# Projection weights of a two-layer encoder: one split per layer kept in DRAM and reloaded as pairs, against a split at each use

## The chip, the cores and the metric

The kernel runs on one core of one Trainium2 chip. The metric is the device time of one execution in microseconds (us); a lower time is better.

## What is computed

Two sequences (x_prompt and x_sample, 1024 tokens of width 1024 each) go through the same two layers. Per layer:

```
(shift, scale, gate) = silu(c) @ W_ada + b_ada
h = RMSNorm_pre(x) * (1 + scale) + shift
P = h @ W_in                      # 1024 -> 32 tiles of 128 columns
A: latent attention, B: RWKV-7, C: Mamba-2 SSD, D: gated DeltaNet   # four mixers on columns of P
x = x + gate * RMSNorm_post(concat(A, B, C, D) @ W_out)
```

All arrays are float32. The weights of a layer are the same for both sequences.

## The kernel before, in words

There are four units of work, (sequence 0, layer 0), (1, 0), (0, 1), (1, 1). Each has an input projection (`stage_in`), four mixers (`mixers`) and an output projection (`stage_out`; the last unit's is `stage_out_last`). While the mixers of one unit run, the projections of its neighbours are spread between them: `ahead`, `behind` and `spread` give their instructions a priority in the middle of the mixers', and a scheduler then writes each engine's queue. Every engine, and SP, which issues all DMAs, works through its own queue in order.

The projections are done in float32 accuracy with three float32r matmuls per block: each operand is the sum of a high part (rounded to float32r) and a low part (the rest). For the activations these are hh and hl, made once per half of a sequence. For the weights they are wh and wl. `in_tile` (line 302) makes one tile of P, 128 columns of W_in by 512 tokens (half `hf`): for each half of the contraction (4 blocks of 128 rows) a tile w of 128 x 512 float32 (256 KB) is loaded (line 309), ScalarE (ACT) casts it to wh (line 327) and VectorE (DVE) subtracts to wl (line 329), both of them in `split_w` and with raised priority (`urgent`). Twelve matmuls follow (line 458, in `paced`), hh by wh, hl by wh, hh by wl for each of the four blocks. `out_tiles` (line 332) does the same for W_out with 256 columns per matmul. w has two buffers, wh and wl three each (GB, GL).

`paced` ties each run of 5 (TK) or 8 (TO) of these matmuls to a memset of a token on GpSimd (line 462), which the next run waits for.

A tile of P, `st`, goes to DRAM; the mixers load it from there (G, cvi, zz and others). Lines that the prediction speaks of: the convolution of mixers C and D is line 638 (DVE, cva) with 634 and 636 (ACT), its activation 640 (ACT, cvt), and 1025 squares it for the norm in D, whose sums PE takes with line 590.

Each weight tile is used four times per layer, by two sequences and two halves. So there are 2 layers x 32 tiles x 2 halves of the contraction x 4 uses = 512 loads and splits for W_in, and 2 x 4 column blocks x 4 x 4 = 128 for W_out, 640 in all. By W_D, W_B and W_REST the 32 tiles of W_in are dealt in three parts; each unit runs the parts for one half of the sequence and then for the other. The stretches of the trace that the prediction names are W_REST (19 tiles) of four parts: 339 to 529 us of sequence 0 in layer 0 (first use of these tiles), 1318 to 1487 of sequence 1 in layer 0, 2581 to 2732 of sequence 0 in layer 1 (first use), 3729 to 3892 of sequence 1 in layer 1. The place from 3660 to 3680 us lies in the parts before the last of these.

Of the kernel before, what the change touches and what calls it, by code (L numbers as in the profile page):

```python
# [21 lines left out]
D = 1024  # L22
MIX = 1800
EA = 60
GK = 4
GB = 3
EB = 60
TK = 5
TO = 8
ED = 90  # L30
GL = 3
SB = 3
NPT = 8
EC = 60
T = 1024
# [73 lines left out]
class Body:  # L109
    def __init__(self, ctx, tc, A, outs, sl=None):  # L110
        self.tc, self.nc, self.A, self.outs = tc, tc.nc, A, outs
        self.n = 0
        self.side = "left"
        self.span = None
        nc = tc.nc
        self.cp = ctx.enter_context(tc.tile_pool(name="cp", bufs=1))
        self.dr = ctx.enter_context(tc.tile_pool(name="dr", bufs=1, space=DRAM))
        self.banks = 3
        self.held = None
        self.token = self.t(self.cp, [1, 1], tag="token")  # L120
        self.gate, self.run = None, 0
        self.ident = self.const(self.cp, "ident")
        self.blk = self.const(self.cp, "blk")
        self.bsel = self.const(self.cp, "bsel")
        self.cc = self.t(self.cp, [128, 4], tag="cc")
        nc.vector.memset(self.cc[:, 0:1], -0.5)
        nc.vector.memset(self.cc[:, 1:2], EPS)
        nc.vector.memset(self.cc[:, 2:3], 0.5)
        nc.vector.memset(self.cc[:, 3:4], 1.0)
        self.mhalf, self.eps, self.phalf, self.one1 = (self.cc[:, i:i + 1] for i in range(4))  # L130
# [127 lines left out]
                    for j in range(2):  # L258
                        nc.vector.tensor_scalar(L.gsc[:, k0 + j, :], ps2[:, 2 * j:2 * j + 2], 1.0, L.pp("gpre", k0 + j), ADD, MUL)

    def stage_in(self, s, L, l, xsrc, Pd, parts=((0, W_ORDER), (1, W_ORDER))):

        for hf, names in parts:
            if self.held is None or self.held[0] != (Pd, hf):
                self.spread()
                hh = self.t(self.pj, [128, 8, 512], F32R, tag="hh")
                hl = self.t(self.pj, [128, 8, 512], F32R, tag="hl")
                self.norm_in(s, L, xsrc, hf, hh, hl)
                self.held = (Pd, hf), hh, hl
            for name in names:  # L270
                self.spread()
                self.in_tile(l, name, hf, *self.held[1:], Pd)
# [28 lines left out]
    def in_tile(self, l, name, hf, hh, hl, Pd):  # L301
# [3 lines left out]
        ps = self.t(self.pps, [128, 512], tag="pj")  # L305
        for k in range(8):
            if k % 4 == 0:
                w = self.t(pj, [128, 4, 128], tag="w", bufs=2)
                self.dma(w, self.A["w_in"][l, ci][:, k * 128:k * 128 + 512].rearrange("p (k c) -> p k c", k=4))
            if k % GK == 0:  # L310
                with self.urgent():
                    wh, wl = self.split_w(w[:, k % 4:k % 4 + GK], [128, GK, 128])
            for i, (a, b) in enumerate(((wh, hh), (wh, hl), (wl, hh))):
                self.paced(TK, ps[0:M], a[:, k % GK, 0:M], b[:, k, :], dict(start=(k == 0 and i == 0), stop=(k == 7 and i == 2)))
        st = self.t(pj, [128, 512], tag="st", bufs=SB)
        with self.urgent():
            if name[0] == "z":
# [3 lines left out]
                nc.scalar.copy(st[0:M], ps[0:M])  # L321
        self.dma(Pd[ci * 128:ci * 128 + M, hf * 512:(hf + 1) * 512], st[0:M])

    def split_w(self, w, shape):
        nc, pj = self.nc, self.pj
        wh = self.t(pj, shape, F32R, tag="wh", bufs=GB)
        nc.scalar.copy(wh, w)  # L327
        wl = self.t(pj, shape, F32R, tag="wl", bufs=GL)
        nc.vector.tensor_tensor(wl, w, wh.bitcast(F32), SUB)  # L329
        return wh, wl  # L330

    def out_tiles(self, l, ch, hh, hl, kqs, at=lambda kq: kq):

        nc, pj = self.nc, self.pj
        pss = [self.t(self.pps, [128, 2, 256], tag="pj") for _ in range(2)]
        for n, kq in enumerate(kqs):
            w = self.t(pj, [128, 2, 256], tag="w", bufs=2)
            self.dma(w, self.A["w_out"][l, ch, kq // 2][:, (kq % 2) * 512:(kq % 2) * 512 + 512].rearrange("p (k c) -> p k c", k=2))
            with self.urgent():
                wh, wl = self.split_w(w, [128, 2, 256])  # L340
            for i in range(4):
                ps = pss[i // 2][:, i % 2]
                c = slice(i * 128, (i + 1) * 128)
                for k in range(2):
                    a, b = hh[:, at(kq) * 2 + k, c], hl[:, at(kq) * 2 + k, c]
                    first, last = n == 0 and k == 0 and i % 2 == 0, n == len(kqs) - 1 and k == 1
                    for m, (u, w2) in enumerate(((a, wh), (a, wl), (b, wh))):
                        self.paced(TO, ps, u, w2[:, k], dict(start=first and m == 0, stop=last and m == 2, skip_group_check=True))
        return pss

    def stage_out(self, s, L, l, xsrc, od, dst):
# [1253 lines left out]
    def full(self):  # L1605
# [11 lines left out]
        def run_in(u, *parts):  # L1617
            s, l = units[u]
            if u not in P:
                P[u] = self.t(self.dr, [NWT * 128, 1024], tag="P", bufs=2)  # L1620
            self.stage_in(s, L[l], l, src(s, l), P[u], parts)

        def run_out(u):
            s, l = units[u]
# [20 lines left out]
        def out_last(parts, ctx=None):  # L1645
            s, l = units[3]
            self.stage_out_last(s, L[l], l, src(s, l), o[3], self.outs[s], parts, ctx)

        early = (0, W_D + W_B), (1, W_D + W_B)
        late = (1, W_REST), (0, W_REST)  # L1650
        with ExitStack() as io:
# [62 lines left out]

# [12 lines left out]
```

## Time and profile before

| | us |
|---|---|
| three runs: median (lowest to highest) | 4856.7 (4849.28 to 4880.52) |
| the profiled execution | 4863.89 |
| its span, first to last instruction | 4862.1 |
| mean granted TensorE clock in it | 0.877 of full speed |

The trace is of one execution. Names are those of the program without buffer numbers; L458 is line 458. A line can be that of a helper: line 144 is every DMA issue, line 458 every paced matmul, of which pj<-hh,wl and its like belong to the input projection. SP's DMA queue is called SPq. A busy time of PE contains the latency of its matmuls, which overlap. A wait is put down to what came last.

### The profile page before, as it was taken

To read this page: it belongs to the slowest core of one execution; us is meant where nothing else is said; L and a number is where in the kernel's file an instruction comes from. 1 tells how busy PE (TensorE), PEld (TensorE's weight loads), DVE (VectorE), ACT (ScalarE), POOL (GpSimd) and SP (SyncE) were. 2 spreads that over 40 slices of the span, in tenths; PEclk is the share of its full clock that TensorE was granted. 3 is DMA by queue.
4 is the path that set the end of the run, shared out by engine and by line. 5 is a ranking of instruction groups with operands and counts; after the bars stand their busy time and mean duration, and the time that the engine had idled before them with its cause. 6 is when DMAs were issued, how large, how long until landed. Compare 5 with 4: busy or idle time off the path is not lost.

```text
span 4862.1 us, 100716 instructions
## 1 busy us (share of the span) xinstructions
PE 4303.3 (89%) x38644; PEld 3243.0 (67%) x38644; DVE 3351.1 (69%) x6837; ACT 2177.4 (45%) x4734; POOL 399.5 (8%) x2093
## 2 busy tenths in 40 slices
PE   6879798999898988998989898898989988889985
PEld 3657565767676775764767666775767766767675
DVE  2488878567688886555549869767556969857466
ACT  2444364554435453531554454454445254446233
POOL 0111010000101110000011100000011100000000
PEclk8889898998998897988989799797989988878688
DMA  4444364343543455453445354644245345365233
GB/s 146 136 146 143 99 196 145 100 114 117 164 148 121 144 162 158 129 152 100 138 144 164 113 166 132 197 140 135 70 149 177 129 135 157 111 200 146 75 100 127
DMA packets 495063, 671.79 MB, mean 138 GB/s; under 512 B 149752, under 2 KB 265976, under 8 KB 493560
## 3 DMA queue, kind: packets, MB, share of 16 engines
q1 hardware_dynamic: 494584, 665.36, 43.9%
q8 instruction: 306, 5.01, 0.4%
q14 instruction: 173, 1.42, 0.1%
HBM read 486.53 MB, written 178.57 MB: 137 GB/s over the span
## 4 chain that ended last, share of the span: by engine, by line
PE 58%; DVE 16%; DMA 14%; issue 5%; ACT 5%; SPq 1%; POOL 1%; DVEq 0%; POOLq 0%; ACTq 0%
PE pj L458 27%; PE b L824 2%; DVE iA L522 2%; PE b L1570 2%; PE b L551 2%; DMA w<-w_in 2%; PE pj L243 2%; PE b L557 1%; PE b L1557 1%; DVE wl L329 1%; DVE GT L537 1%; SPq L144 1%; PE y L1222 1%; PE b L1526 1%; PE b L590 1%
## 5 line engine op out<-in xcount | busy, mean ns | idle before, releaser
L458 PE MATMUL pj<-hh,wl 128*128 128x512 f32 (+1 forms) x2048 | 849.4, 415 | 41.9 <-DVE wl L329 28.8
L458 PE MATMUL pj<-hh,wh 128*128 128x512 f32 (+1 forms) x2048 | 854.2, 418 | 25.8 <-POOL token L462 10.2
L458 PE MATMUL pj<-hl,wh 128*128 128x512 f32 (+1 forms) x2048 | 847.4, 414 | 18.3 <-POOL token L462 18.2
L327 ACT CAST wh<-w 128x512 fp32r<-128x512 f32 x640 | 395.6, 618 | 782.6 <-PE pj L458 523.8
L329 DVE TENSOR_TENSOR wl<-w,wh 128x512 fp32r<-128x512 f32 x640 | 447.3, 700 | 253.3 <-ACT wh L327 211.7
L458 PEld LDWEIGHTS pj<-hh,wl 128*128 128x128 f32 (+1 forms) x2048 | 397.2, 194 | 148.1 <-DVE wl L329 27.6
L458 PEld LDWEIGHTS pj<-hh,wh 128*128 128x128 f32 (+1 forms) x2048 | 398.0, 194 | 128.8 <-POOL token L462 16.1
L458 PEld LDWEIGHTS pj<-hl,wh 128*128 128x128 f32 (+1 forms) x2048 | 397.8, 194 | 113.9 <-POOL token L462 26.3
L462 POOL MEMSET token<- 1x1 f32 x1613 | 143.4, 89 | 3347.0 <-PE pj L458 3342.1
L458 PE MATMUL pj<-wh,hl 128*128 128x256 f32 x896 | 270.7, 313 | 1.3 <-DVE hl L363 1.2
L1561 ACT ACTIVATE pT<-b 128x512 f32<-128x512 f32 x256 | 150.7, 598 | 262.7 <-PE b L1559 258.2
L458 PE MATMUL pj<-wh,hh 128*128 128x256 f32 x768 | 236.2, 308 | 11.5 <-ACT st L372 5.9
L458 PE MATMUL pj<-wl,hh 128*128 128x256 f32 x768 | 231.5, 302 | 3.7 <-DVE wl L329 3.7
L294 PE MATMUL pj<-c_ident,x 128*128 128x128 f32 x416 | 120.4, 393 | 122.0 <-DVE x L289 43.9
L1527 DVE TENSOR_REDUCE mx<-b 128x1 f32<-128x512 f32 x256 | 169.9, 684 | 84.1 <-PE b L1526 82.4
L638 DVE SCALAR_TENSOR_TENSOR cva<-cvi,cw,cva 128x1024 f32<-128x1024 f32 x144 | 183.7, 1278 | 46.8 <-ACT cva L634 33.8
L458 PEld LDWEIGHTS pj<-wh,hl 128*128 128x128 f32 x896 | 182.8, 208 | 17.5 <-issue 9.7
L1570 PEld LDWEIGHTS b<-VO,pT 128*64 128x64 f32 x4096 | 152.8, 144 | 52.1 <-issue 43.9
L1570 PE MATMUL b<-VO,pT 128*64 128x65 f32 x4096 | 182.5, 233 | 0.9 <-ACT pT L1561 0.9
L824 PE MATMUL b<-AR,BK 64*64 64x128 f32 x2048 | 178.4, 305 | 3.5 <-DVE G L829 3.2
L829 DVE SCALAR_TENSOR_TENSOR G<-b,Dk,mk 128x128 f32<-128x128 f32 x512 | 140.7, 341 | 53.2 <-PE b L824 52.8
L296 ACT ACTIVATE ht<-pj,shc,gsc 128x256 f32<-128x256 f32 x208 | 118.6, 570 | 126.8 <-PE pj L294 63.2
(403 smaller groups left out, 9125.1 us busy)
## 6 DMA issues: line engine op xcount, KB each, us to landing
w<-w_in SPq DMA_DIRECT2D x512, 256.0 KB
P<-st SPq DMA_DIRECT2D x248, 256.0 KB
x<-x SPq DMA_DIRECT2D x76, 512.0 KB
w<-w_out SPq DMA_DIRECT2D x128, 256.0 KB
G<-P SPq DMA_DIRECT2D x112, 256.5 KB
cvi<-P SPq DMA_DIRECT2D x48, 512.0 KB
f<-acr SPq DMA_DIRECT2D x32, 512.0 KB
bkc<-bkd SPq DMA_DIRECT2D x64, 256.0 KB
```

The costliest lines, as they stand in the source:

```text
L294: nc.tensor.transpose(ps[:, i * 128:(i + 1) * 128], xs[i][:, k * 128:(k + 1) * 128], self.ident)
L296: nc.scalar.activation(ht, ps[:, 0:256], AF.Identity, scale=L.gsc[:, k, s:s + 1], bias=L.shc[:, k, s:s + 1])
L327: nc.scalar.copy(wh, w)
L329: nc.vector.tensor_tensor(wl, w, wh.bitcast(F32), SUB)
L458: m = self.nc.tensor.matmul(*mm[:3], **mm[3]).ins
L462: t = self.nc.gpsimd.memset(self.token, 0.0).ins
L638: nc.vector.scalar_tensor_tensor(a, c[:, j:j + 1024], wt(j, i), a, MUL, ADD)
L824: nc.tensor.matmul(pss[x][self.half(x ^ a), i * 128:i * 128 + 128], BK[self.half(x), pr, c, a], AR[self.half(x), pr, c].rearrange("p a t - ...
L829: v.scalar_tensor_tensor(G[:, x, pr, c, :], pss[x][:, i * 128:i * 128 + 128], Dk[:, c, 2 * x + pr:2 * x + pr + 1], mk, MUL, MUL)
L1527: v.tensor_reduce(mx[:, n, qt:qt + 1], ps, AX.X, ALU.max, negate=True)
L1561: nc.scalar.activation(pT[kt], ps, AF.Exp)
L1570: nc.tensor.matmul(po[64 * x:64 * x + 64, i, :], pT[kt][:, o:o + 64], VO[:, kt, h, :], start=(kt == 0 and i == 0), stop=(kt == 7), skip_gr ...
```

## The change

`split_w` is replaced by `halves`. The first time that a half tile of a weight is used, w is loaded and split as before, but into one tile w2 that holds both parts (128 x 2 x 512, 512 KB), and w2 is then also written to a DRAM tile (`win`, `wout`). At the other three uses the pair is loaded from there into w2 and no engine splits anything. w2 has six buffers (WB = 6), 24 KB per partition, in the place of three wh and three wl (12 KB); w keeps two. The matmuls read w2[:, 0] for wh and w2[:, 1] for wl; their count and shapes stay. `dynamic_dma_scratch_size` of 1024 is passed at the creation of the program, where nothing was passed before. `stage_in` has a path that writes hh and hl to DRAM and loads them back; the set `twice` that selects it is empty, and no such DMA is in the program.

In counts: casts and subtractions 640 before, 160 after; loads of w 640 before, 160 after; loads of pairs 0 and 480; writes of pairs 0 and 160.

```diff
@@ constants @@
-GK = 4
-GB = 3
-GL = 3
+WB = 6
@@ Body.__init__ @@
+        self.kept = {}
+        self.wd = {(n, l): self.t(self.dr, [m, 128, 2, 512], tag=f"w{n}{l}") for l in range(DEPTH) for n, m in (("in", 2 * NWT), ("out", 16))}
+        self.spilled = {}
@@ in_tile @@
             if k % 4 == 0:
-                w = self.t(pj, [128, 4, 128], tag="w", bufs=2)
-                self.dma(w, self.A["w_in"][l, ci][:, k * 128:k * 128 + 512].rearrange("p (k c) -> p k c", k=4))
-            if k % GK == 0:
-                with self.urgent():
-                    wh, wl = self.split_w(w[:, k % 4:k % 4 + GK], [128, GK, 128])
-            for i, (a, b) in enumerate(((wh, hh), (wh, hl), (wl, hh))):
-                self.paced(TK, ps[0:M], a[:, k % GK, 0:M], b[:, k, :], dict(start=(k == 0 and i == 0), stop=(k == 7 and i == 2)))
+                w2 = self.halves(("in", l, ci, k // 4), lambda: self.A["w_in"][l, ci][:, k * 128:k * 128 + 512]).rearrange("p u (k c) -> p u k c", k=4)
+            for i, (a, b) in enumerate(((0, hh), (0, hl), (1, hh))):
+                self.paced(TK, ps[0:M], w2[:, a, k % 4, 0:M], b[:, k, :], dict(start=(k == 0 and i == 0), stop=(k == 7 and i == 2)))
...
-    def split_w(self, w, shape):
+    def halves(self, key, src):
         nc, pj = self.nc, self.pj
-        wh = self.t(pj, shape, F32R, tag="wh", bufs=GB)
-        nc.scalar.copy(wh, w)
-        wl = self.t(pj, shape, F32R, tag="wl", bufs=GL)
-        nc.vector.tensor_tensor(wl, w, wh.bitcast(F32), SUB)
-        return wh, wl
+        w2 = self.t(pj, [128, 2, 512], F32R, tag="w2", bufs=WB)
+        wf = w2.bitcast(F32)
+        if key in self.kept:
+            self.dma(wf, self.kept[key])
+            return w2
+        w = self.t(pj, [128, 512], tag="w", bufs=2)
+        self.dma(w, src())
+        with self.urgent():
+            nc.scalar.copy(w2[:, 0], w)
+            nc.vector.tensor_tensor(w2[:, 1], w, wf[:, 0], SUB)
+        kept = self.wd[key[:2]]
+        self.kept[key] = kept[key[2] * 2 + key[3]] if key[0] == "in" else kept[key[2] * 4 + key[3]]
+        self.dma(self.kept[key], wf)
+        return w2
@@ out_tiles @@
-            w = self.t(pj, [128, 2, 256], tag="w", bufs=2)
-            self.dma(w, self.A["w_out"][l, ch, kq // 2][:, (kq % 2) * 512:(kq % 2) * 512 + 512].rearrange("p (k c) -> p k c", k=2))
-            with self.urgent():
-                wh, wl = self.split_w(w, [128, 2, 256])
+            w2 = self.halves(("out", l, ch, kq), lambda: self.A["w_out"][l, ch, kq // 2][:, (kq % 2) * 512:(kq % 2) * 512 + 512]).rearrange("p u (k c) -> p u k c", k=2)
...
@@ full, kernel @@
+        twice = set()
-    nc = bacc.Bacc("TRN2", target_bir_lowering=False, num_devices=1)
+    nc = bacc.Bacc("TRN2", target_bir_lowering=False, num_devices=1, dynamic_dma_scratch_size=1024)
```

Line numbers after the change are higher by 1 at the DMA issue (145) and by 14 from `out_tiles` on (458 is 472, 640 is 654, 1025 is 1039).

The first place is ACT's queue in the last unit (sequence 1, layer 1), in the convolution of mixer D, while the projection tiles W_D and W_B of half 1 are spread between: cva and cvt are of the convolution, st is a tile of P leaving PSUM. Before:

```order
L321 COPY st_37871<-pj_37829 128x512
L634 ACTIVATE cva_40263<-cvi_40259,cw_15_114 128x1024
L327 CAST wh_37942<-w_37940 128x512
L327 CAST wh_37967<-w_37965 128x512
L321 COPY st_37916<-pj_37874 128x512
L640 ACTIVATE cvt_40268<-cva_40263 128x1024
L1024 COPY KQ_40084<-cva_40263 128x16x64
L1025 ACTIVATE cvt_40268<-cva_40263 128x1024
L327 CAST wh_37987<-w_37985 128x512
```

After:

```order
L648 ACTIVATE cva_38539<-cvi_38535,cw_19_118 128x1024
L328 COPY st_36544<-pj_36510 128x512
L654 ACTIVATE cvt_38544<-cva_38539 128x1024
L1038 COPY KQ_38360<-cva_38539 128x16x64
L1039 ACTIVATE cvt_38544<-cva_38539 128x1024
L328 COPY st_36581<-pj_36547 128x512
```

The casts are gone from this place, and the rest stands in the same order.

The second place is SP's queue in the same part of the program: w and win are weights, P_..<-st_.. stores a tile of P, cvi loads one for the convolution. Before:

```order
L144 DMA w_37761<-w_in 128x512
L144 DMA P_36722<-st_37692 128x512
L144 DMA w_37786<-w_in 128x512
L144 DMA cvi_40161<-P_36722 128x1024
L144 DMA w_37806<-w_in 128x512
L144 DMA P_36722<-st_37737 128x512
L144 DMA w_37830<-w_in 128x512
```

After:

```order
L145 DMA w_5338_36454<-win_3_62 128x1024
L145 DMA P_35510<-st_36360 128x512
L145 DMA w_5341_36474<-win_3_62 128x1024
L145 DMA cvi_38437<-P_35510 128x1024
L145 DMA w_5342_36491<-win_3_62 128x1024
L145 DMA P_35510<-st_36397 128x512
L145 DMA w_5345_36511<-win_3_62 128x1024
```

The weights stand where they stood among the other transfers, each twice as long. The running numbers tell how far ahead of the tile being stored a load stands: a tile of P takes 45 numbers before and 37 after, so w_37761 beside st_37692 is about 1.5 tiles ahead, and w_36454 beside st_36360 about 2.5.

The third place is SP's queue in the first stage, where the first tiles are split. Before:

```order
L144 DMA w_500<-w_in 128x512
L144 DMA w_521<-w_in 128x512
L144 DMA w_545<-w_in 128x512
L144 DMA hl_228<-w_ada 128x1024 x2
L144 DMA ht_205<-b_ada 2x256
```

After:

```order
L145 DMA win_1_60<-w_117_459 128x1024
L145 DMA w_505<-w_in 128x512
L145 DMA win_1_60<-w_119_480 128x1024
L145 DMA w_526<-w_in 128x512
L145 DMA win_1_60<-w_123_504 128x1024
L145 DMA w_550<-w_in 128x512
L145 DMA hl_232<-w_ada 128x1024 x2
L145 DMA ht_209<-b_ada 2x256
```

Each load of w now has the write of an earlier pair ahead of it.

On PE the matmuls of the projections stand at most some 130 places (of 9216) earlier or later among the mixers' instructions than they did, except in the last 1500 instructions of the mixers, where up to 250 come later and, at the very end, some 130 earlier.

## Rows read from the trace of the kernel before

**Rows 1.** Page, section 1: engine, busy us (share of span), x instructions.
```profile
span 4862.1 us, 100716 instructions
...
PE 4303.3 (89%) x38644; PEld 3243.0 (67%) x38644; DVE 3351.1 (69%) x6837; ACT 2177.4 (45%) x4734; POOL 399.5 (8%) x2093
```

**Rows 2.** Chain that ended last, whole program: by engine, then by line.
```profile
PE 58%; DVE 16%; DMA 14%; issue 5%; ACT 5%; SPq 1%; POOL 1%; DVEq 0%; POOLq 0%; ACTq 0%
...
by line: PE pj L458 27.1%; issue 4.8%; PE b L824 2.2%; DVE iA L522 2.2%; PE b L1570 2.0%; PE b L551 1.8%; DMA w<-w_in 1.8%; PE pj L243 1.8%; PE b L557 1.4%; PE b L1557 1.3%; DVE wl L329 1.3%; DVE GT L537 1.3%; SPq L144 1.3%; PE y L1222 1.2%
```

**Rows 3.** Page, section 5: the split's groups and their first reader.
```profile
L458 PE MATMUL pj<-hh,wl 128*128 128x512 f32 (+1 forms) x2048 | 849.4, 415 | 41.9 <-DVE wl L329 28.8
...
L327 ACT CAST wh<-w 128x512 fp32r<-128x512 f32 x640 | 395.6, 618 | 782.6 <-PE pj L458 523.8
L329 DVE TENSOR_TENSOR wl<-w,wh 128x512 fp32r<-128x512 f32 x640 | 447.3, 700 | 253.3 <-ACT wh L327 211.7
```

**Rows 4.** Waits, whole program: us in total, times, longest us.
```profile
ACT wh L327 <- PE pj L458: 523.8, 280, 9.2
...
DVE wl L329 <- ACT wh L327: 211.7, 165, 9.3
ACT wh L327 <- DMA w<-w_in: 180.2, 91, 8.8
```

**Rows 5.** Waits of SP's DMA queue, whole program, same columns.
```profile
SPq L144 <- DVE wl L329: 580.7, 232, 23.2
```

**Rows 6.** Timeline of ACT, 3660 to 3680: start, us, instruction [idle before].
```profile
3672.53 0.62 ACT L327 CAST wh<-w 128x512 fp32r<-128x512 f32 x1 [3.94 <-PE pj L458]
...
3673.53 1.06 ACT L640 ACTIVATE cvt<-cva 128x1024 f32<-128x1024 f32 x1
...
3676.84 1.05 ACT L1025 ACTIVATE cvt<-cva 128x1024 f32<-128x1024 f32 x1
```

**Rows 7.** Timeline of DVE, then of PE, same stretch and columns.
```profile
3668.86 0.68 DVE L329 TENSOR_TENSOR wl<-w,wh 128x512 fp32r<-128x512 f32 x1
3669.47 2.60 DVE L638 SCALAR_TENSOR_TENSOR cva<-cvi,cw,cva 128x1024 f32<-128x1024 f32 x2
...
3677.94 2.30 PE L590 MATMUL b<-cc,cvt 64*64 64x1 f32 x40 [3.66 <-ACT cvt L1025]
```

**Rows 8.** Windows: length, busy us (instructions) per engine, PEclk, DMA share, GB/s.
```profile
339.00:529.00 190.00, 183.25 (x1604) 145.09 (x1602) 160.87 (x312) 81.79 (x179) 20.27 (x108) 0.95 0.43 140
1318.00:1487.00 169.00, 150.50 (x1040) 118.68 (x1038) 146.75 (x261) 68.96 (x127) 13.72 (x110) 0.92 0.49 152
2581.00:2732.00 151.00, 143.01 (x940) 111.73 (x938) 143.99 (x244) 53.87 (x82) 22.72 (x107) 1.00 0.49 152
3729.00:3892.00 163.00, 150.56 (x1025) 120.20 (x1024) 156.49 (x250) 56.55 (x86) 21.25 (x108) 0.94 0.47 144
```

**Rows 9.** The chain by line in 1318 to 1487, then in 3729 to 3892.
```profile
by line: PE pj L458 34.7%; DMA w<-w_in 17.6%; issue 7.4%; DVE GT L537 5.4%; PE b L1304 3.4%; SPq L144 3.4%; PE b L1066 2.8%; PE b L1292 2.8%; PE b L551 2.7%; DVE wl L329 2.5%; ACT wh L327 2.2%; DVE iA L522 2.2%; PE w L1179 1.4%; PE b L557 1
...
by line: PE pj L458 40.5%; DVE GT L537 5.6%; PE b L1066 5.3%; DVE iA L522 5.2%; issue 4.5%; DVE wl L329 4.2%; PE b L1304 4.0%; PE yd L1349 3.8%; PE b L551 2.3%; DMA f<-acr 2.3%; DVE f L1330 2.2%; PE cb L1323 2.2%; DVE iT L529 1.8%; POOL f L
```

**Rows 10.** Line 329 alone in 3729 to 3892: its DVE busy us (instructions).
```profile
3729.00:3892.00 163.00, 27.74 (x38) 0.94 0.47 144
```

**Rows 11.** Page, sections 2, 3, 6: DMA packets, queue, weight issues.
```profile
DMA packets 495063, 671.79 MB, mean 138 GB/s; under 512 B 149752, under 2 KB 265976, under 8 KB 493560
...
q1 hardware_dynamic: 494584, 665.36, 43.9%
...
w<-w_in SPq DMA_DIRECT2D x512, 256.0 KB
...
w<-w_out SPq DMA_DIRECT2D x128, 256.0 KB
```

**Rows 12.** Two weight loads on the chain: start us, us, piece.
```profile
1313.74 3.82 DMA w<-w_in
...
1322.21 10.41 DMA w<-w_in
```

More of the change, by code (lines that the diff above doesn't have):

```diff
@@ L259, in ada, with stage_in @@
                         nc.vector.tensor_scalar(L.gsc[:, k0 + j, :], ps2[:, 2 * j:2 * j + 2], 1.0, L.pp("gpre", k0 + j), ADD, MUL)
-    def stage_in(self, s, L, l, xsrc, Pd, parts=((0, W_ORDER), (1, W_ORDER))):
-        for hf, names in parts:
+    def stage_in(self, s, L, l, xsrc, Pd, parts, again):
+        for n, (hf, names) in enumerate(parts):
             if self.held is None or self.held[0] != (Pd, hf):
@@ L267, in stage_in @@
                 hl = self.t(self.pj, [128, 8, 512], F32R, tag="hl")
-                self.norm_in(s, L, xsrc, hf, hh, hl)
+                back = self.spilled.get((s, l, hf))
+                if back is None:
+                    self.norm_in(s, L, xsrc, hf, hh, hl)
+                    if again[n]:
+                        self.spilled[s, l, hf] = back = self.t(self.dr, [2, 128, 4096], tag="hd", bufs=2)
+                        for i, h in enumerate((hh, hl)):
+                            self.dma(back[i], h.bitcast(F32).rearrange("p k t -> p (k t)"))
+                else:
+                    for i, h in enumerate((hh, hl)):
+                        self.dma(h.bitcast(F32).rearrange("p k t -> p (k t)"), back[i])
                 self.held = (Pd, hf), hh, hl
@@ L346, in out_tiles @@
                     first, last = n == 0 and k == 0 and i % 2 == 0, n == len(kqs) - 1 and k == 1
-                    for m, (u, w2) in enumerate(((a, wh), (a, wl), (b, wh))):
-                        self.paced(TO, ps, u, w2[:, k], dict(start=first and m == 0, stop=last and m == 2, skip_group_check=True))
+                    for m, (u, x) in enumerate(((a, 0), (a, 1), (b, 0))):
+                        self.paced(TO, ps, u, w2[:, x, k], dict(start=first and m == 0, stop=last and m == 2, skip_group_check=True))
         return pss
@@ L1620, in run_in @@
                 P[u] = self.t(self.dr, [NWT * 128, 1024], tag="P", bufs=2)
-            self.stage_in(s, L[l], l, src(s, l), P[u], parts)
+            self.stage_in(s, L[l], l, src(s, l), P[u], parts, [(u, hf) in twice and names[0] == W_D[0] for hf, names in parts])
         def run_out(u):
```

## The prediction

> **What bounds the kernel now.** I read the engines' busy times first, then the chain of work that ended last, then the waits, then two stretches in detail. No engine is full: PE is busy for 89% of the span by records that include the latency of each matmul, DVE for 69%, ACT for 45% [rows 1]. The chain says how the rest comes about: 58% of the span is PE, 16% DVE, 14% DMA, 5% ACT, 5% issue, so a good third of the time is spent in hand-overs between engines that run their queues in order [rows 2]. On that chain stand the pieces of the weight path itself: the load of w (1.8%) and the subtraction for wl (1.3%), besides the cast to wh, which lies below the last share listed (1.2%) [rows 2].
>
> The weight path costs little on PE: the matmuls that read wl stood idle 28.8 us for it in the whole program [rows 3]. It costs more on the engines that split. The cast waits 523.8 us for PE to give back a wh buffer and 180.2 us for its load; the subtraction waits 211.7 us for the cast [rows 4]; and SP's queue waits 580.7 us for the subtraction to free a w buffer [rows 5]. All four queues are in order, so what stands behind a waiting cast is late with it. Rows 6 and 7 show one case: the cast at 3672.53 ended 3.94 us of ACT idling; the cvt of line 640 ran behind it at 3673.53, though its input cva had been complete at 3672.07; the cvt of line 1025 followed at 3676.84, and PE, which had waited 3.66 us, began on it at 3677.94 [rows 6, 7]. Without the cast that cvt could have started 1.46 us sooner, and some 0.6 us more if the subtraction at 3668.86 had not stood ahead of the cva on DVE: 1.46 to 2.1 of 3.94 us come back, 37 to 54%.
>
> In some stretches DVE itself is the bound: from 3729 to 3892 it is busy 156.5 of 163 us, from 1318 to 1487 146.8 of 169 [rows 8]. Of the first, 27.7 us are subtractions for wl [rows 10].
>
> **The change, part by part.**
>
> *Splits that go.* Of 640 casts and 640 subtractions 160 stay. 480 x 618 ns = 297 us leave ACT, 480 x 700 ns = 336 us leave DVE [rows 3]. Most of that is beside PE's work. On the path stand w and wl: (1.8% + 1.3%) x 4862 = 151 us, of which three quarters go, 113 us. For the cast I take 19 us; its bounds are 0 and three quarters of 58 us, that is 44. Together -132 us.
>
> *DVE-full stretches.* The chain counts only 4.2% of 163 us, 6.8 us, of subtractions in 3729 to 3892 [rows 9], but with DVE 96% busy all 27.7 us [rows 10] are on its queue: about 21 us more. In 1318 to 1487 the stage has the same tiles and so about as much, of which the chain holds 2.5%, 4 us [rows 9]; DVE is 87% busy there, and I count 14 us. Together -35 us; bounds 0 and -44.
>
> *Loads that double.* The queue moved 665.36 MB in 43.9% of the span [rows 11], that is 312 GB/s while the DMA engines were busy, so 256 KB take 0.84 us of them and 512 KB 1.68 us. Added are 480 x 0.84 = 403 us and 160 writes x 1.68 = 269 us: 672 us, which lifts the share from 43.9% to 57.7%. A pair needs to be there only six half tiles later, so no load is late by its size alone; the price falls on the other transfers. These make 14% - 1.8% = 593 us of the chain [rows 2], about 150 legs at some 4 us, if the 3.82 us of a plain weight load is a fair size [rows 12]. A leg that arrives at random now meets a weight transfer 538 us / 4862 = 11% of the time and waits half of 0.84 us, on the mean 0.05 us. Afterwards weight transfers make 480 x 1.68 + 160 x 2.52 = 1210 us, 25%, half of one is 0.84 us, on the mean 0.21 us. So +0.16 us x 150 = +24 us. Bounds: 0, and one whole pair ahead of each leg, 252 us; I stay with the value from the queue's own rate.
>
> The Trainium skill (DMA: Bandwidth & Descriptors, section Anatomy of one DMA) fits a transfer issued by GpSimd as a fixed 2.0 us plus bytes over 436 GB/s; by that a pair would hold the engines 0.6 us longer than a single tile and not 0.84, and the 24 us would be 12, while the rows' own rate is the lower one and is what I use.
>
> *Stretches where the split remains.* The first use of each tile keeps its split and adds a write of 512 KB. In 2581 to 2732, the 38 half tiles of W_REST in layer 1, that is 38 x 1.68 = 64 us, 0.42 on top of a share of 0.49 [rows 8]: 0.91. In 339 to 529 it is 0.77. The load of the next w stands behind that write, with two w buffers as before. The shares stay under 1, so I charge a quarter of a microsecond for each of 160 writes: +40 us. Bounds 0 and 269 us. The read-back of a tile comes at the earliest a whole part of the projection later (7 or more tiles), so it does not wait for its write.
>
> *SP's waits.* A pair's load waits for PE to release the pair six before it; the w load waited for DVE, and that, through cast and wh, for PE five half tiles back. Behind it on SP stand the same stores and loads of the mixers as before; in the order that the change section shows, the load stands beside the P store of a tile farther back than it did. I take 0; the bounds are 0 and what the second rival below from this cause costs. The shorter list of splits leaves the projection matmuls on PE where they were, except near the end of the last mixers, where up to 250 of them come later and some 130 of the last ones earlier; I take 0 for that; with half of the 415 ns of a 512-column record [rows 3] as an estimate for one of 256 columns, the bounds are -27 us (130) and +52 us (250).
>
> *Scratch and spill.* All DMA issues of the profile are on SP, and the set that would turn the spill of hh and hl on is empty, so both cost nothing. The Trainium skill (SBUF — State Buffer, section SBUF size) calls the scratch the ring of descriptors that GpSimd writes; no run here shows what a smaller one does.
>
> **Sum.** -132 - 35 + 24 + 40 = -103 us. The profiled execution took 4863.9 us (span 4862.1), so 4761 us; the median of the runs shown, 4856.7, lies 7 us below it, and I predict 4754 us. Its own range, from halving and raising the four terms by half, is 4705 to 4805.
>
> **Rivals.** *More comes back.* The 19 us for the cast would be too little if holds like that of rows 6 and 7 delay PE more often than the chain, a single path, shows. Three quarters of 523.8 us [rows 4] at 37 to 54% are 145 to 212 us; with half of the middle on the path another 89 us go: 4665 us. For it speaks that 280 casts waited so; against it, that the chain holds less than 58 us of casts.
>
> *Hidden anyway.* Where the weight path was last, something else is nearly as late: PE works through its queue in order and line 458 alone has 27.1% of the chain. If half of the 132 goes, and 15 of the 35: -66 - 15 + 24 + 40 = -17 us, 4840 us. For it speaks that PE waited only 28.8 us for wl.
>
> *Slower: the DMA legs of the mixers.* SP's one queue would hold loads twice as long, each waiting for PE, and the mixers' transfers behind them would land later: P, G, cvi, f. Row 12 shows it in little: one weight load took 3.82 us, the next, in a crowd, 10.41 us. If the 593 us of other legs stretch by 35%, 208 us take the place of the 24: -167 + 208 + 40 = +81 us, 4938 us. Against no change it decides from (167 - 40) / 593 = 21%, and for 1% more from 30%. Against it: a mean share of 57.7%, and loads that stand singly between other transfers.
>
> That the change does not do what it says I leave out: the order shows 160 casts in place of 640 and 480 loads of pairs.
>
> **How the numbers follow.** Forecast 0.45, more comes back 0.17, hidden 0.24, slower 0.14. The likeliest gives 4754 us. Faster by over 1% (below 4808; a per cent is about what a measurement of this kernel tells from no change) are nearly all of the forecast, the first rival and a sixth of the second: 0.64. Within 1% lie most of the second and the edges: 0.22. Slower: 0.14. The range 4630 to 4890 leaves out the better part of the slower rival and the outer end of the first, about 0.16.
>
> **What would show it.** Right: casts 160 and about 99 us, subtractions 160 and about 112 us; the wait of casts for PE down from 523.8 to below 150 us; SP waiting for PE at line 472 instead of DVE; no weight load over 1% of the chain; the stage that runs from 3729 to 3892 with about 129 us of DVE work in place of 156.5; DMA share near 0.58. Wrong, if PE's matmuls wait for pair loads for more than some 30 us, if the chain's DMA share rises above 18%, or if the first-use stages grow by more than 40 us together.

## The result and the profile after the change

| | us |
|---|---|
| kernel before, median of the runs beside it (lowest to highest) | 4854.32 (4849.28 to 4880.52) |
| changed kernel, median of 4 runs (lowest to highest) | 4938.1 (4914.83 to 4944.75) |
| ratio, with its 95% interval | 1.0153 (1.0111 to 1.0196) |
| the profiled execution, its span, its mean granted clock | 4944.75, 4943.0, 0.872 |

The change costs 1.5%; the forecast was 4754 us, with a range of 4630 to 4890, and both were wrong. The page of the changed kernel, section 1, against [rows 1]:

```profile
span 4943.0 us, 99399 instructions
...
PE 4369.7 (88%) x38644; PEld 3268.0 (66%) x38644; DVE 3073.8 (62%) x6357; ACT 1912.4 (39%) x4254; POOL 395.0 (8%) x2093
```

DVE lost 277 us of work and ACT 265; the split's own groups fell by 333 and 297 us, as worked out. PE has the same 38644 matmuls, and is busy for 66 us more. The splits that stay, and the copy of a finished tile of P out of PSUM, in the same page's section 5, against [rows 3]:

```profile
L328 ACT COPY st<-pj 128x512 f32<-128x512 f32 (+1 forms) x192 | 111.8, 582 | 386.1 <-PE pj L472 351.8
...
L342 ACT CAST w<-w 128x512 fp32r<-128x512 f32 x160 | 98.9, 619 | 229.0 <-DMA w<-w_in 133.3
L343 DVE TENSOR_TENSOR w<-w,w 128x512 fp32r<-128x512 f32 x160 | 113.8, 712 | 108.9 <-ACT w L342 104.2
```

The waits of ACT in the changed kernel (us in total, times, longest), against [rows 4]:

```profile
ACT st L328 <- PE pj L472: 351.8, 114, 24.9
...
ACT st L325 <- PE pj L472: 162.3, 42, 17.4
ACT w L342 <- DMA w<-w_in: 133.3, 65, 7.8
...
ACT bkc L897 <- DMA bkc<-bkd: 100.2, 50, 9.1
...
ACT G L746 <- DMA G<-P: 73.1, 39, 5.9
ACT w L342 <- PE pj L472: 63.1, 29, 7.4
ACT st L385 <- PE pj L472: 53.3, 14, 28.8
```

and the same three copies to st in the kernel before:

```profile
ACT st L321 <- PE pj L458: 52.3, 36, 4.2
...
ACT st L318 <- PE pj L458: 26.9, 14, 4.7
...
ACT st L371 <- PE pj L458: 12.1, 12, 2.4
```

The cast's wait for PE fell from 523.8 to 63.1 us, which the prediction gave as a sign of success. But the copies to st now wait 567 us for PE (351.8 + 162.3 + 53.3), where they waited 91: ACT's in-order queue stands before PE as long as it did, one instruction further on. The 133.3 us that casts still wait for their loads fall on 160 casts; the 180.2 of [rows 4] fell on 640. SP's queue waits for PE in the place of DVE [rows 5]; of its three longest waits the second was there before (220.2 us, for line 294):

```profile
SPq L145 <- PE pj L472: 917.7, 376, 16.8
SPq L145 <- PE pj L305: 219.5, 27, 49.9
SPq L145 <- DVE w L343: 141.8, 60, 10.0
```

The DMA rows of the page, against [rows 11]: the share is 56.1% where 57.7% was worked out.

```profile
DMA packets 518093, 881.44 MB, mean 178 GB/s; under 512 B 152312, under 2 KB 268536, under 8 KB 516600
...
q1 hardware_dynamic: 517624, 875.08, 56.1%
...
w<-win SPq DMA_DIRECT2D x384, 512.0 KB
win<-w SPq DMA_DIRECT2D x128, 512.0 KB
```

**Where the time went.** The 29428 matmuls outside the projections can be counted off in both traces, and the start of the n-th compared. The profiled run is late by 21 us at the 1200th (448 us into the run before), by 45 at the 3600th (838 us), 51 at the 4800th (939) and 98 at the 6000th (1103). Read every 1200 matmuls, it then stays between 70 and 108 late, but for a dip to 20 near 4600 us, and ends 86 late. At the 1200th, 3600th and 6000th both kernels have the same number of projection matmuls behind them (within one); at the 4800th the changed one has done 30 fewer, some 12 us of work. How far such a reading can be trusted is shown by a run of the kernel before with nothing changed but the scratch (below): it differs by 1 to 5 us up to 939, by 16 at 1103 and by up to 41 later. So most of the loss is made in the first unit; of the rest no more can be said by this. The windows of the changed kernel that hold the worst of it (columns as in [rows 8]) and, last, the one with the tiles of 3729 to 3892:

```profile
1099.00:1201.00 102.00, 102.00 (x540) 61.20 (x541) 23.27 (x80) 24.10 (x44) 2.85 (x12) 0.64 0.12 37
...
1151.00:1185.00 34.00, 34.00 (x169) 19.36 (x168) 6.91 (x24) 7.47 (x15) 0.00 (x0) 0.50 0.00 1
...
3837.00:4031.00 194.00, 179.52 (x1417) 141.66 (x1415) 157.84 (x272) 43.21 (x79) 20.52 (x108) 0.93 0.62 191
```

Before, the stretch between the same two points of the count ran from 1058 to 1103:

```profile
1058.00:1103.00 45.00, 45.00 (x508) 30.21 (x509) 21.22 (x67) 28.00 (x54) 2.88 (x5) 1.00 0.11 37
...
1074.00:1088.00 14.00, 14.00 (x177) 9.70 (x180) 4.30 (x15) 4.90 (x9) 1.37 (x2) 1.00 0.23 76
```

PE is recorded as full in both. Some 500 matmuls took 102 us in the one and 45 in the other, and the DMA engines were idle for nine tenths of it in both. The 45 us are the lower of two values. The run with only the scratch changed has the same order, and there the stretch between the same points of the count took 57 us, at a lower clock:

```profile
1062.34:1118.92 56.58, 56.58 (x509) 36.16 (x509) 21.79 (x69) 28.60 (x55) 3.35 (x5) 0.76 0.09 29
```

So up to 12 us of the difference can be the clock's; the five traces of the changed order have 96 to 103 us here. In the middle of the 102 us, 169 matmuls took 34 us, with the clock granted at 0.50 of full speed, its level of 1.2 GHz. PE's timeline there (start, us, instruction) shows what it was fed:

```profile
1149.75 0.68 PE L838 MATMUL b<-AR,BK 64*64 64x128 f32 x2
1150.36 0.48 PE L1584 MATMUL b<-VO,pT 128*64 128x65 f32 x2
1150.77 0.69 PE L305 MATMUL pj<-c_ident,x 128*128 128x128 f32 x2
...
1156.34 0.68 PE L838 MATMUL b<-AR,BK 64*64 64x128 f32 x2
1156.95 0.48 PE L1584 MATMUL b<-VO,pT 128*64 128x65 f32 x2
1157.36 0.68 PE L838 MATMUL b<-AR,BK 64*64 64x128 f32 x2
```

Line 838 (824 before) is a product of the RWKV mixer on a 64x64 part of the array, line 1584 (1570 before) the weighted sum of values in attention, on 128x64; the scheduler laid two of one and two to four of the other in turn, with transposes on the whole array (line 305) here and there. What a turn costs can be read in the kernel before, on its chain from 1080 to 1120 (start, us, piece), at the full clock:

```profile
1079.96 0.26 PE b L1570 x2
1080.22 0.36 PE b L824 x2
1080.58 0.26 PE b L1570 x2
...
1083.05 0.73 PE b L1570 x18
...
1091.05 0.80 PE b L824 x12
```

Two and two in turn take 0.62 us. In unbroken rows 0.73/18 and 0.80/12 are the time of one, and two and two take 0.21 us. So, as an estimate from these pieces, each change costs some 0.2 us at the full clock. At the lower one two and two take 1.02 us (1156.34 to 1157.36 above). Counted in the order of PE's queue, where a matmul of the one line follows directly on one of the other, the kernel before has 118 such changes (33, 81, 2 and 2 in the four units), the changed one 231 (101, 56, 2 and 72), and both have the same 2048 matmuls of the one line and 4096 of the other. The Trainium skill (TensorEngine Tiling (Array Packing), section Key Properties) says that a change of the tiling mode, not merely of the tile, drains TensorE. It gives no price; these rows agree with it and have one.

### The profile page after: what moved, and what is told of

It reads as the page before. It is cut to its first block, busy times and chain, and to the rows that moved or that the text cites. A ratio compares the mean times of both kernels' runs of the same rounds, so it can differ in the third digit from the quotient of the medians.

```text
span 4943.0 us, 99399 instructions
## 1 busy us (share of the span) xinstructions
PE 4369.7 (88%) x38644; PEld 3268.0 (66%) x38644; DVE 3073.8 (62%) x6357; ACT 1912.4 (39%) x4254; POOL 395.0 (8%) x2093
## 3 DMA queue, kind: packets, MB, share of 16 engines
q1 hardware_dynamic: 517624, 875.08, 56.1%
## 5 line engine op out<-in xcount | busy, mean ns | idle before, releaser
L472 PE MATMUL pj<-hh,w 128*128 128x512 f32 (+1 forms) x4096 | 1439.6, 423 | 52.3 <-POOL token L476 21.4
L472 PEld LDWEIGHTS pj<-hh,w 128*128 128x128 f32 (+1 forms) x4096 | 790.6, 197 | 264.6 <-POOL token L476 34.6
L472 PE MATMUL pj<-hl,w 128*128 128x512 f32 (+1 forms) x2048 | 860.7, 421 | 21.9 <-POOL token L476 13.8
L472 PEld LDWEIGHTS pj<-hl,w 128*128 128x128 f32 (+1 forms) x2048 | 404.4, 197 | 119.7 <-POOL token L476 20.2
L472 PE MATMUL pj<-w,hh 128*128 128x256 f32 x1536 | 344.4, 313 | 11.0 <-ACT st L386 8.4
L472 PEld LDWEIGHTS pj<-w,hh 128*128 128x128 f32 x1536 | 273.0, 210 | 35.8 <-issue 15.9
L472 PE MATMUL pj<-w,hl 128*128 128x256 f32 x960 | 265.1, 309 | 10.4 <-ACT hl L438 7.3
L328 ACT COPY st<-pj 128x512 f32<-128x512 f32 (+1 forms) x192 | 111.8, 582 | 386.1 <-PE pj L472 351.8
L652 DVE SCALAR_TENSOR_TENSOR cva<-cvi,cw,cva 128x1024 f32<-128x1024 f32 x144 | 183.7, 1281 | 58.4 <-ACT cva L648 42.8
L472 PEld LDWEIGHTS pj<-w,hl 128*128 128x128 f32 x960 | 185.8, 208 | 21.4 <-ACT hl L438 7.7
L342 ACT CAST w<-w 128x512 fp32r<-128x512 f32 x160 | 98.9, 619 | 229.0 <-DMA w<-w_in 133.3
L343 DVE TENSOR_TENSOR w<-w,w 128x512 fp32r<-128x512 f32 x160 | 113.8, 712 | 108.9 <-ACT w L342 104.2
L838 PEld LDWEIGHTS b<-AR,BK 64*64 64x64 f32 x2048 | 122.0, 147 | 70.0 <-issue 49.6
```

Source lines behind the costliest of these rows:

```text
L343: nc.vector.tensor_tensor(w2[:, 1], w, wf[:, 0], SUB)
L472: m = self.nc.tensor.matmul(*mm[:3], **mm[3]).ins
L652: nc.vector.scalar_tensor_tensor(a, c[:, j:j + 1024], wt(j, i), a, MUL, ADD)
L838: nc.tensor.matmul(pss[x][self.half(x ^ a), i * 128:i * 128 + 128], BK[self.half(x), pr, c, a], AR[self.half(x), pr, c].rearrange("p a t - ...
```

## The experiments

Theories: *order* (the new order of PE's queue costs the time), *bytes* (the pairs' 210 MB delay other transfers), and, for the term on the other side, what the *splits* were worth. Where only bytes or the size of a split were to change, instructions were edited after the scheduler had written the queues, so that order, waits and buffers stayed. All ratios are to the kernel before, run beside them, with 95% intervals.

**Half the bytes of the pair loads.** The matmuls read the high half of a pair for the low one. In words:

```diff
+ for each load of a pair (source win, wout):  512 of 1024 columns
+ for each matmul on w2[:, 1]:                 read w2[:, 0]
```

> The changed program with every queue in the same order, but each of the 480 pair loads brings only its high half (256 KB in place of 512), and the matmuls take the high half where they took the low one; that part of the sum is left out. DMA-traffic theory: the doubled loads are what delays the mixers' transfers, so at least half of the 84 us that the change lost comes back, 4900 us or less. Queue-order theory: the loss comes from the order in which the scheduler wrote PE's queue where the attention and RWKV mixers of the first unit meet (the stretch from 1100 to 1200 us, with 101 changes between the two in place of 33); the order is the same here, so the time stays within 15 us of the changed kernel, 4925 to 4950 us.

Measured: 4892.74 us, 1.006 (1.0031 to 1.0088). Over half of the loss is back (1.0138 in the next run to 1.006), with the loads at the size they had before.

**The changed kernel once more**, as the measure for the runs that follow.

> The changed kernel itself, on the chip and beside the kernel before of this batch, as the measure for the three others. Every theory: a ratio to before of 1.011 to 1.020 (4915 to 4945 us if before takes 4860). It also separates chance from cause: if the ratio here were below 1.006, the half loads of the first batch would have won nothing.

Measured: 4939.31 us, 1.0138 (1.0093 to 1.0184).

**Half loads and half writes.** As above, and each write of a pair is cut to 512 columns too.

> The changed kernel in its own order of instructions, where the pair loads and the pair writes move only the high half (256 KB in the place of 512 KB each; the matmuls read the high half for the low one, so the output is another). With the loads alone cut the ratio was 1.006. Theory A, the bytes of the writes delay the stages of first use (the +20 us in the first 450 us): cutting 160 x 256 KB, 131 us of transfer at the 312 GB/s of the engines when busy, of which a sixth shows, takes another 15 to 30 us: 4860 to 4875 us, ratio 1.000 to 1.003, and the first 450 us are at most 8 us later than in before. Theory B, the writes are hidden and the first 450 us are late by the order of the instructions: ratio 1.004 to 1.008 as with the loads alone, and the +20 us stay.

Measured: 4879.15 us, 0.9996 (0.9972 to 1.002). The 1200th matmul is 8 us later than before, where it was 19 to 21 in the changed kernel: theory A.

**The bytes of before, without splits.** All later loads bring the high half of one pair of their layer, and 156 of 160 writes are 8 columns wide.

> The changed kernel in its own order, where 156 of the 160 pair writes move 8 columns and four move the high half, and the later uses load the 256 KB of one pair of their layer (the output is another). So the bytes are within 1 MB those of before, the splits are gone and the order stays. Theory A, the writes cost what half of them won, twice: from 1.006 with half loads and full writes by 2 x 0.0064 to 0.993 (0.990 to 0.996). Theory B, the writes are hidden: 1.003 to 1.008. Against e3_short_splits (0.988 with the order of before) what is left over is the order's: 0.5% to 1.8%.

Measured: 4873.04 us, 1.0006 (0.9977 to 1.0035), between the theories. From half loads (1.006) the writes gave 0.5%, all of it already with the first half cut. Two waits of ACT in this run:

```profile
ACT w L343 <- DMA w<-w_in: 65.3, 35, 6.6
...
ACT G L747 <- DMA G<-P: 51.7, 26, 6.9
```

They were 133.3 and 73.1 with the pairs' bytes, which delayed first loads and loads of G. The wait for bkc, 100.2 there, is 103.3 here, so that one was not the bytes'. With the bytes of before and 480 splits fewer the kernel is no faster than before; something that is neither bytes nor splits eats what the splits gave.

**Before, with loads doubled.** The second to fourth load of a weight tile brings 1024 columns, the upper 512 read by nothing (474 loads, 124 MB; w is twice as wide, and the scratch is 1024 bytes to make room).

> The kernel before, all instructions in the same order, with 474 of its 640 weight loads (the second to fourth use of a tile) bringing 512 KB in the place of 256 KB; the upper half is read by nothing. It adds 124 MB, where the changed kernel adds 126 MB by its pair loads and 84 MB by its writes. Theory A, bytes on the queues delay the other loads: the half loads won 0.8% against the changed kernel, so this loses as much: ratio 1.006 to 1.010, spread over the whole span. Theory B, the loads are hidden and the changed kernel lost by its order alone: ratio 0.998 to 1.002.

Measured: 4969.2 us, 1.0221 (1.0172 to 1.0271), more than either theory gave. Against 180.2 us in [rows 4] its waits say:

```profile
ACT wh L328 <- DMA w<-w_in: 301.4, 131, 10.0
```

The 121 us more stand beside 107 us of loss (0.0221 x 4856.5). In the changed kernel an equal 126 MB of loads cost 0.8%. There a pair waits in one of six buffers; here w has two and a cast behind it. That the buffers make the difference was not tried by itself.

**Before, with short splits.** At the later uses of W_in (384 of the 480) the cast and the subtraction do 8 columns of 512, and the matmuls read activations for the weights.

> The kernel before with every queue in the same order and the same loads, but at the second to fourth use of each tile of W_in the cast and the subtraction do 8 of 512 columns and the matmuls read columns of their activations for the weights, so the result leaves the true weights out there. 384 x 2 instructions shrink, some 200 us on ACT and 240 us on DVE. My prediction's chain term (three quarters of 151 us, and 35 us of stretches full on DVE): 90 to 150 us faster, about 4740 us. Rival, the splits were hidden behind PE anyway: less than 30 us faster, 4825 us or more.

Measured: 4811.41 us, 0.9878 (0.9827 to 0.9929), 59 us of 4869, between the two theories; in proportion 74 us for all 480, which is an estimate, as W_out's splits were not tried and the short ones still take 195 and 170 ns. Groups of line 328 by form, and the wait:

```profile
L328 ACT CAST wh<-w 128x512 fp32r<-128x512 f32 x256 | 158.3, 619 | 285.0 <-PE pj L459 201.0 <-DMA w<-w_in 56.6 <-DMA w<-w_out 9.1
...
L328 ACT CAST wh<-w 128x8 fp32r<-128x8 f32 x384 | 75.0, 195 | 556.5 <-PE pj L459 385.9 <-DMA w<-w_in 121.7 <-issue 17.8
```

The casts are short and wait for PE for 587 us (201.0 + 385.9), longer than the 523.8 of before. The gain is slow and spread: against the run with only the scratch changed, in the same order, 7 us at 838, 34 at 2661, 53 at 4059 and 50 at the end. (Against the profiled run of before it reads 6, 16, 21 and 42; that run alone loses some 27 us from 4477 to 4597.)

**The changed kernel with RWKV first in unit 0.** The scheduler puts an instruction of smaller priority earlier.

```diff
             self.tc.cur_priority = p[self.side]
+            self.tc.cur_priority += -200 * (m == "b" and od is self.od0)
             getattr(self, "mixer_" + m)(L, Pd, l, od)
```

> The changed kernel with the RWKV mixer of the first unit given a priority 200 places ahead, which the scheduler turns into 13 changes between attention and RWKV matmuls on PE in the first unit in place of 101 (13, 13, 1, 18 in the four units in place of 101, 56, 2, 72); loads, splits and counts are the same. Queue-order theory: 50 us or more come back, 4890 us or less. DMA-traffic theory: the time stays within 20 us of 4938 us.

Measured: 4871.26 us, 1.0004 (0.997 to 1.0039). The 53 us that had gone between the 3600th and the 6000th matmul are back (it is 44 late at the one and 46 at the other), with all pairs and bytes in place. 45 changes are left of 231. The half loads came out as the traffic theory had it and this run as the order theory had it, so each of the two is a part of the loss.

**Before, with another order** (EA = 64 in the place of 60, which sets how far into the first mixers the rest of the first projection is spread): 100, 37, 1 and 3 changes.

> The kernel before with the constant EA at 64 in place of 60, which spreads the projection of the second unit a little differently and turns the 33 changes between attention and RWKV matmuls in the first unit into 100 (100, 37, 1, 3 in the four units in place of 33, 81, 2, 2); no other code differs. Queue-order theory: the first unit loses some 40 us and the second gains part of it, 4870 to 4910 us, without a single changed DMA. DMA-traffic theory: within 15 us of the kernel before.

Measured: 4888.55 us, 1.0025 (0.9992 to 1.0059). In its trace the 6000th matmul is 27 us late (the 3600th is 7), which is where unit 0's changes fall, and the last one 6. The interval holds no change as well as the 0.2 to 0.3% that 23 more changes would cost.

**Before, with RWKV first in unit 0.** The same line of code in the kernel before: 0, 1, 1 and 1 changes.

> The kernel before, with the RWKV mixer of the first unit 200 steps ahead in the scheduler's priorities. The matmul queue then changes between attention's and RWKV's 64-row matmuls 0, 1, 1 and 1 times in the four units, where before does 33, 81, 2 and 2 times. Theory A, that alternation costs what the changed kernel lost at 1099 to 1201 us: about 0.5 us for each change in a stretch where nothing else runs, 33 and 81 of them partly beside other work: 10 to 40 us less than before, ratio 0.992 to 0.998. Theory B, the order moves work inside the mixers and the end is set by the sum of the work: ratio 0.998 to 1.004. If it is over 1.004, the order is paid for elsewhere.

Measured: 4808.33 us, **0.987 (0.9838 to 0.9902)**, faster than both kernels, and more than expected.

**Before, with RWKV first in all units.** `-200 * (m == "b")`: 0, 67, 54 and 2 changes.

> The kernel before with the RWKV mixer 200 steps ahead in all four units, not in the first alone. Here the matmul queue changes between attention and RWKV 0, 67, 54 and 2 times in the units: 123 in all, where before has 118 and e6_before_rwkv_first had 3. Theory A, what e6_before_rwkv_first won (ratio 0.987) came from the alternation that went, some 0.5 us for each change: ratio 0.997 to 1.004, with the stretches of units 1 and 2 where the queue alternates slow. Theory B, it came from RWKV going ahead, whatever the alternation: ratio 0.982 to 0.991.

Measured: 4860.75 us, 1.0006 (0.9983 to 1.0029): theory A. The two lines on PE in the mixers of unit 2, first with RWKV first in unit 0 alone (3215 to 3391, one change), then in all units (3229 to 3455, 54 changes):

```profile
L824 PE MATMUL b<-AR,BK 64*64 64x128 f32 x256 | 25.3, 382 | 0.6 <-DVE G L829 0.6
...
L1570 PE MATMUL b<-VO,pT 128*64 128x65 f32 x512 | 17.5, 233 | 0.0
```

```profile
L824 PE MATMUL b<-AR,BK 64*64 64x128 f32 x256 | 40.6, 415 | 0.0
L1570 PE MATMUL b<-VO,pT 128*64 128x65 f32 x512 | 37.1, 268 | 0.0
```

The same 768 matmuls keep PE for 77.7 us in the place of 42.8, part of it by the clock, which is 0.77 in the first window and 0.68 in the second. Counted by matmuls, this run falls back against the one with RWKV first in unit 0 alone by 35 us between the 19800th and the 20400th, where the 54 changes lie, and by 22 between the 12600th and the 13200th, where the 67 of unit 1 lie; 20 of the 22 are back by the 15000th. At each of these counts both runs have the same number of projection matmuls behind them.

**Both cures.** The changed kernel with RWKV first in unit 0, and half loads and half writes.

> The changed kernel with both cures: the RWKV mixer of the first unit 200 steps ahead (changes between attention and RWKV 13, 13, 1 and 18), and pair loads and writes of the high half alone (256 KB each, the output is another). Theory A, bytes and order are two costs that add up: the order took the changed kernel from 1.0138 to 1.0004, the half pairs from 1.0138 to 0.9996, both together give 0.986 (0.983 to 0.990), about 4805 us. Theory B, they are one cost seen twice (with the order mended, the bytes fall into time that waits anyway): 0.995 to 1.000.

Measured: 4794.72 us, 0.9855 (0.9816 to 0.9895): theory A. Order and bytes add up.

**Before, with the small scratch alone** (`dynamic_dma_scratch_size=1024`).

> The kernel before with the dynamic DMA scratch cut to 1024 bytes and nothing else, all instructions in the same order. Theory A, the scratch is used by no transfer of this kernel: ratio 0.998 to 1.002. Theory B, a part of the changed kernel's loss comes from the small scratch (descriptors that wait for space): ratio above 1.004, and waits of POOL or SP grow in the trace.

Measured: 4871.68 us, 0.9993 (0.9965 to 1.0021): no effect.

All the kernels with their whole weights or their order changed, by the number of changes and PE's busy time on the two lines:

| kernel | changes | PE busy on the two lines, us | ratio |
|---|---|---|---|
| before | 118 | 182.5 + 178.4 = 360.9 | 1 |
| before, RWKV first in unit 0 | 3 | 156.6 + 157.1 = 313.7 | 0.987 |
| before, RWKV first in all units | 123 | 203.4 + 173.8 = 377.2 | 1.0006 |
| before, EA = 64 | 141 | 191.8 + 171.7 = 363.5 | 1.0025 |
| changed (its second run) | 231 | 204.3 + 211.4 = 415.7 | 1.0138 |
| changed, RWKV first in unit 0 | 45 | 175.8 + 158.6 = 334.4 | 1.0004 |
| changed, no bytes more than before | 231 | 200.7 + 205.8 = 406.5 | 1.0006 |
| changed, RWKV first, half pairs | 45 | 174.6 + 154.3 = 328.9 | 0.9855 |

From 3 changes to 231 PE's time on these lines grows by 102 us, some 0.45 us a change.

The first unit can be compared by itself. At the 1200th, the 3600th and the 6000th matmul outside the projections all runs have the same number of projection matmuls behind them (within one; 10 more at the 1200th with EA = 64), and all changes of unit 0 but 6 of EA = 64 lie between the last two. The times between them, in us:

| order of PE's queue, runs | changes | 1200th to 3600th | 3600th to 6000th |
|---|---|---|---|
| of before: profiled run, short splits, small scratch, loads doubled | 33 | 391, 390, 391, 408 | 265, 265, 279, 279 |
| before, RWKV first in unit 0, in all units | 0 | 398, 396 | 263, 270 |
| before, EA = 64 | 94 | 397 | 284 |
| changed: two runs, half loads, half loads and writes, no bytes more | 101 | 415, 412, 412, 411, 406 | 317, 312, 311, 314, 307 |
| changed, RWKV first: whole pairs, half pairs | 13 | 419, 407 | 267, 267 |

In the second stretch 101 changes take 307 to 317 us whatever the bytes, and 0 or 13 take 263 to 270. With EA = 64 94 of them take only 284, so a change has no one price. In the first stretch, which has none, the changed order takes 15 us longer than that of before even with the bytes of before (406 against 391). No run changed the alternation alone: a new order moves other work too.

## Why the prediction was wrong

**The step that failed** is in the part on SP's waits: the shorter list of splits "leaves the projection matmuls on PE where they were, except near the end of the last mixers", and "I take 0 for that". The scheduler's order does change elsewhere. The projections stay in their stages (though by the n-th matmul of the traces they are up to 333 places off, near the 25100th, and not 130), but inside the mixers of units 0 and 3 attention and RWKV are dealt out in turn where they had run in blocks: 138 changes more, and 25 fewer in unit 1, 113 in sum. Going from 231 changes to 45 gave 1.34% with full pairs and 1.41% with half ones, 65 to 69 us for 186 changes or 0.36 us each; going from 118 to 3 gave 63 us, 0.55 each. So the 113 cost some 41 to 62 us, as an estimate at these mean prices, and PE's busy time on the two lines, 50 to 55 us longer, fits it. The bounds set for that 0, -27 and +52, came from matmuls of the projections and were nearly wide enough by chance. They were also narrow by the page of before: a matmul of 256 columns has a mean of 302 to 313 ns there, not 207.

**Splits that go, and the DVE-full stretches** (-132 and -35): the right sign and over twice the size. Short splits in the order of before give 74 us in proportion. The chain's share of the load and the subtraction was taken as time that comes back. But PE was what came next: the ACT queue that held at the cast now holds at the copy to st, for matmuls of the same line (567 us against 91), and the casts cut to 195 ns wait longer than the long ones did. The case of [rows 6] and [rows 7] leaves out the line of ACT that ran between the cast and the cvt:

```profile
3673.06 0.58 ACT L321 COPY st<-pj 128x512 f32<-128x512 f32 x1
```

Such copies wait for PE too (the 91 us above) and stay after the change, so it was not shown that the 1.46 us would come back with the cast alone. The stretch of 3729 to 3892, in which DVE was to do 129 us of work in place of 156.5, comes out as a window of 194 us with 157.84 us of DVE in it, because more of the mixers' work fell into it; PE has 1417 matmuls there where it had 1025.

**Loads that double and writes** (+24 and +40): the sum of 64 was met, but by luck, as the parts were not. Loads cost 0.78% (1.0138 to 1.006), 38 us; writes 0.54% (1.006 to 1.0006), 26 us. The rate of 312 GB/s held: 639 us more of the queue's time (56.1% of 4943 less 43.9% of 4862) against the 672 worked out. Of the signs named as wrong, the first-use stages grew by 21 us in the first 450 us and by 24 from 2581 to 2732 (151 us) to 2668 to 2843 (175), just over the 40. The first is the writes' (8 with half of them, none with 8 columns); the second stretch also holds 1193 matmuls where it had 940, so its 24 us are not all a cost. PE waited for no pair load that shows among its longer waits. The chain after the change could not be followed back beyond 5% of PE in this trace, so its DMA share and that of the weight loads stay unread.

**Scratch and spill** (0): right, 0.9993 for the scratch alone.

**The sum with the measured terms**: -74 + 38 + 26 + 41 to 62 = +31 to +52 us, where 67 (0.0138 x 4872.6) and 74 (0.0153 x 4854.3) were measured. 15 to 43 us are left, and by the intervals of the ratios each measured term is uncertain by 20 to 30. Part of the rest can be seen. Before the first change between attention and RWKV, from the 1200th to the 3600th matmul, the changed order already takes 15 us longer with the bytes of before and without the splits (406 against 391), and putting RWKV first does not bring that back. The run without more bytes gives the whole in another way: it is 3 us slower than before with 74 us of splits gone, so what is neither split nor byte in the change, its order and the six buffers together, costs some 77 us. What in the order makes the 15 us, and whether the buffers have a part, is not shown and stays open.

**The rivals.** "Slower: the DMA legs of the mixers" gave 4938 us, to the microsecond the median, and by luck: it put 208 us on the mixers' transfers and 40 on the writes, where loads and writes cost 64 together, and nothing on PE's order. Its mechanism is seen in small (G, and the first loads behind the writes). "Hidden anyway" was right about the splits: it counted 66 and 15 us for them, 81, where 74 were measured.

## What to carry to other kernels

Where a scheduler writes the queues, an edit in one engine's work can redeal all of them; compare the order inside the stages that the edit does not touch, and count how often PE's queue changes between matmuls of different tile shapes. A new order can cost or give more than the edit: here one line of priority gave 1.3%, and the edit without it lost as much. Before splits or casts are traded for bytes, look at what the engine that does them would wait for next: if it is PE, the wait can move on to the next instruction and only a part comes back, while the added bytes can delay the loads behind them.

## What was not expected of the hardware

A PE recorded as busy for 102 of 102 us did about half of what it could: 540 matmuls, many of them two of one tile shape and two to four of another in turn, took that long at a granted clock of 0.64, and the 508 of the kernel before took 45 us at 1.00 and 57 us at 0.76. A change between a 64x64 and a 128x64 tile cost some 0.2 us at the full clock by the chain's rows, and some 0.45 us by PE's busy time over whole programs, in which the stretches of alternation also ran with the clock at its lower level: 0.50 for 34 us in the changed kernel, though not from 1074 to 1088 before, where it stayed at 1.00. How much of the 0.45 is the clock's was not taken apart. The busy share shows none of this; only the rows of one shape, and the clock beside them, do.
